# Splitting the second mixer's gated output once, with one token part kept on chip, and new instruction orders at part changes and at the kernel's end

## The chip, the cores and the metric

The kernel runs on one core of a Trainium2 chip. The core has five engines with an instruction stream each: TensorE (PE, the matmuls), VectorE (DVE), ScalarE (ACT), GpSimd (POOL) and SyncE (SP, which here only issues DMAs). They wait for one another through semaphores. POOL and ACT can issue DMAs too. The metric is the device time of one execution in microseconds; the time of a kernel is the median of its runs. Besides these, one execution was recorded by the hardware profiler.

## What is computed

One inference step of a two-layer streaming encoder over 1024 prompt and 32 sample frames (1056 tokens, model width 1024), all in fp32. The first layer mixes by retention, the second by gated linear attention (GLA); each is followed by a feed-forward stage with a causal convolution. Cut to what matters:

```python
for i in range(2):
    h = rmsnorm(x, norm_mix[i])
    if i == 0:
        y, S = retention_mixer(h, ...)   # (silu(g) * groupnorm(o)) @ w_out
    else:
        y, S = gla_mixer(h, ...)         # (silu(r) * rms(o) * norm_g) @ w_out
    x = x + y
    h = rmsnorm(x, norm_ffn[i])
    y, cs = conv_ffn(h, ...)             # (silu(gate) * val) @ w_down after w_up and the convolution
    x = x + y
return rmsnorm(x, norm_final), states
```

In GLA the decay of the keys is a logarithm of a sigmoid of a low-rank product (the "gate features" `a`, 16 wide, times `w_a2`), summed along the tokens.

## The kernel before

**Arithmetic.** An fp32 product is made of three matmuls: each operand is split into a high half, rounded to the engine's faster fp32r type, and a low half, the rest. A split is a copy on ACT (high) and a subtraction on DVE (low). `load_w` does it for weights: a DMA into a `raw` tile (512 KB, 128 x 1024), the copy `whi` and the subtraction `wlo`, both at L102. `Down` (L1187) does it for the other operand: a load into HR (L1221), a copy (L1223), a subtraction (L1224).

**Stages**, in order of time: the retention's input products, its four heads (until 712 us), its output product with w_ro (to about 882), the first feed-forward stage, GLA (1617 to 1947), GLA's output gate (w_gg, to 2039), its output product with w_go (to 2137), the second feed-forward stage and the last norm.

**Retention heads.** A head has eight pieces of prompt tokens and one of sample tokens. For each piece `output` computes the result `po` and its norm: statistics on DVE (L585, L586), a scale from them (L587, root on ACT at L589, L591 to L593), and the scaled result `on` on ACT (L599); `norm` transposes `on` on PE (L604, for the sample the tile is called `or`) and multiplies with the gate (L609). `update` computes the new state `Sn`: matmuls at L621, a DVE instruction at L629. In the last head `Down.early` (L1195) already loads and splits the first two k tiles of w_ro and of its other operand; L546 calls it for the second one.

**Down.** w_ro, w_go and the feed-forward's down product are run by `Down.run` in token parts: `CQ`, four parts of 264 tokens, for w_ro (16 k tiles) and w_go (8 k tiles); `CM`, parts of 384, 384 and 288, for the down product. In each part PE runs over the k tiles, and for each over eight output column tiles `nt`, with three matmuls each (L1248 to L1250). Three weight tiles (`keep`) stay on chip from part to part and are used first in the later parts; the others are loaded and split again in each part. At the last k tile each `nt` is evicted: DVE adds it to the residual (L1424 for w_ro and w_go, L1485 and L1516 for the down product), ACT squares it, and sums of squares are made on DVE and POOL (L148, L215). The norm of a part is computed while PE works on the next part (`hold`: how many k tiles the last column tile waits for its bank).

**Gate and w_go.** `second(1)` first computes, for eight tiles f, the gate product (L1404, `pg`), silu, and the product with GLA's output (L1407), and stores the result to DRAM (`scr_og`). w_go's `Down` reads it back, 32 loads of 132 KB, and splits it there.

**Up-projection.** `ffn_up` forms its products from seven instead of eight block products (numbered m). `weight_sums` and the operand sums (L288, L289, L293, L317 to L323, L312, L313) feed them; each unit's products go to PSUM banks named "a", "b", "c" (line 342), and `put` (L1311) adds them to the output rows. Products 2 and 4 share bank "b".

**Order.** A tile scheduler places the instructions by priority and by what is ready in its model; `order(a, b)` makes `a` stand behind `b`. `later` takes postponed work off a list. Around GLA's start the order follows the program: `qk_products`, `run_tails` (norm of the last part), `closers` (which release the feed-forward's rooms), `qk_out`, then `gates_in` (matmuls L1143 and L1144, feature tile `asb` at L1146 to L1149) and `gate` (L893, L897, L900, scan L902).

**Last norm.** `final_phase` squares the evicted tiles of the last part (L1524), adds them in pairs on POOL (L1528), reduces five tiles on PE (L219), computes the root on DVE and ACT (L225, L164 to L169), scales by `gcol` on ACT (L1511) and by the root on DVE and, for the last pair, POOL (L1537), and stores in four DMAs of 288 KB (L1538).

Of the kernel before, what the change touches and what calls it, by code (L numbers as in the profile page):

```python
# [9 lines left out]
F32 = mybir.dt.float32  # L10
# [40 lines left out]
def trunk_kernel(ctx: ExitStack, tc: tile.TileContext, io):  # L51
# [249 lines left out]
    def seven(X, wsrc, sm, snap_room, begin, put, first):  # L301
# [34 lines left out]
        def product(f, s, i, after):  # L336
            m = first.get((f, s), ORD)[i]
            if i == 0:
                unit[f, s] = {}
                begin(f, s)  # L340
            d = unit[f, s]
            bank = {1: "a", 6: "a", 7: "a", 2: "b", 4: "b", 5: "c", 3: "c"}[m]
            if bank not in d:
                d[bank] = sm("pu")
            ps = d[bank][:, :TH]
            wh, wl = W[f][m]
            x = X[s][m]
            for kt in range(4):
                k = slice(kt * P, kt * P + P)
                mm = PE.matmul(ps, wh[:, k], x[:, 0, kt], start=m in (1, 2, 4, 5) and kt == 0, stop=False,  # L350
                               skip_group_check=True)
# [61 lines left out]
    def retention():  # L413
# [50 lines left out]
        for h in range(RH):  # L464
# [5 lines left out]
            def before(m):  # L470
# [74 lines left out]
                if samp and h + 1 == RH:  # L545
                    d1s[0].early(1, split)  # L546
# [9 lines left out]
            def output(ctx):  # L556
# [20 lines left out]
                else:  # L577
# [9 lines left out]
                V.tensor_scalar(ab[:L, 0:1], mv[:L, 1:2], rcol[:L, h, 3:4], EPS,  # L587
                                op0=ALU.mult, op1=ALU.add)
# [23 lines left out]
                norms.append(norm)  # L612

            def update(ctx):
# [13 lines left out]
                if old is not None:  # L628
                    V.scalar_tensor_tensor(sn, old, float(GAMMA[h] ** L), pu, op0=ALU.mult, op1=ALU.add)  # L629
                else:  # L630
                    S.copy(sn, pu)
                st = sn
                if m >= 7:
                    dst = io["o_ret_p"] if m == 7 else io["o_ret_s"]
                    nc.sync.dma_start(dst[h].rearrange("(d p) e -> p d e", p=P), sn)

# [4 lines left out]
            for ctx in before(7), before(8):  # L641
                output(ctx)
                update(ctx)
# [212 lines left out]
    def gla(closers):  # L856
# [267 lines left out]
        asb = g1.tile([96, T], F32R, tag="asb", name="asb")  # L1124
        p00 = qk_products(0, 0)

# [3 lines left out]
        run_tails(lv)  # L1130
# [20 lines left out]

        units = [(h, c) for h in range(GH) for c in range(3)]
        gates_in(0)
        b00 = gate(*units[0])
# [35 lines left out]
    class Down:  # L1190
        def __init__(self, nk, wsrc, hsrc, chunks, res, sm, keep, hold):
            self.nk, self.wsrc, self.hsrc, self.chunks, self.res, self.sm = nk, wsrc, hsrc, chunks, res, sm
            self.hw = max(n for _, n in chunks)
            self.keep, self.hold, self.kept, self.ops = keep, hold, {}, {}
            self.banks = None  # L1195

        def early(self, kt, after=None):
# [10 lines left out]
            self.ops[0, kt] = load_w(self.wsrc(kt), None, after), (h, h[:, 512:])  # L1208

        def load(self, c, kt):  # L1210
# [16 lines left out]
        def run(self, room, evict, norm_a, norm_b, done, nxt=()):  # L1227
# [3 lines left out]
            for c, (c0, n) in enumerate(self.chunks):  # L1231
# [20 lines left out]
                for i, kt in enumerate(kts):  # L1252
# [118 lines left out]
    def second(l, scr, wg, wo, gncol, ntile, nxt):  # L1371
# [20 lines left out]
        AR = ear.enter_context(pool(f"ar{l}", side="right")).tile([P, 16 * TH + 4 * (T + 4)], F32, tag="AR", name=f"AR{l}")  # L1392
        if wg:
            gn = fp.tile([P, ntile], F32, tag="gn", name=f"gn{l}")
            nc.sync.dma_start(gn, gncol)
            gt = rooms(o=ring(0, T, 3, AR), sg=ring(3 * T, T, 3, AR))
            for f in range(ntile):
# [13 lines left out]
        with pool(f"xh{l}") as xhp, pool(f"xb{l}") as xbp:  # L1411
            XH = xhp.tile([P, 16 * TH], F32R, tag="XH", name=f"XH{l}")
            XB = xbp.tile([P, 32 * TH], F32R, tag="XB", name=f"XB{l}")
# [3 lines left out]
                         kw=ring(8 * TH, 2 * D, 3, XB), hh=ring(0, TH, 8, XH), hl=ring(8 * TH, TH, 8, XH))  # L1417
# [5 lines left out]
            def evict(c, nt, a, ps, ss):  # L1423
                V.tensor_tensor(a, a, ps, op=ALU.add)  # L1424
                sumsq(ss, nt, a, TH)
                c0, n = CQ[c]
                nc.sync.dma_start(scr_x[:, nt, c0:c0 + n], a)

# [80 lines left out]
    def final_phase(down, room, sm):  # L1509
        def scale_g(a, nt):  # L1510
            S.activation(a, a, AF.Copy, scale=gcol[:, 4, nt:nt + 1])  # L1511

        squares = []

        def evict(c, nt, a, ps, ss):
# [17 lines left out]
        def scale(c, xr, kt):  # L1533
            c0, n = CM[c]
            a = xr[:, kt:kt + 2]
            eng = G if c == 2 and kt == 6 else V
            eng.tensor_tensor(a, a, R[:, c0:c0 + n].unsqueeze(1).to_broadcast([P, 2, n]), op=ALU.mult)  # L1537
            (S if c == 2 and kt % 4 else nc.sync).dma_start(io["o_y"][:, kt:kt + 2, c0:c0 + n], a)  # L1538
# [117 lines left out]
_SCRATCH = {"scr_x5": (2, P, 2, 4, TH), "scr_q": (RH - 1, 4, P, 2, 2, TH), "scr_sg": (16, P, T),  # L1656
# [31 lines left out]
```

## Time and profile before

| quantity | value |
|---|---|
| median of 3 runs | 2870.28 us |
| lowest and highest run | 2870.03 and 2872.78 us |
| the profiled execution | 2871.84 us |
| its span, first to last instruction | 2870.1 us |
| mean granted PE clock | 0.996 |
| bytes moved by DMA | 361.40 MB |

A line of the profile names an engine, a source line (L1249), an operation and the tiles it writes and reads (`pd<-hh,whi`). Views used below: busy time of each engine; what an engine waited for; a timeline (start, duration, and in brackets the idle time before it and what released it); groups of instructions (count, busy time, mean in ns); and busy time in stretches of time that one chooses, with the PE clock that was granted.

### The profile page before, as it was taken

How to read it: one execution, taken by the hardware profiler on the slowest of the kernel's cores; microseconds unless marked ns; L12 is line 12 of the kernel's file. 1: busy time of each engine (PE TensorE's matmuls, PEld its weight loads, DVE VectorE, ACT ScalarE, POOL GpSimd, SP SyncE). 2: the span in 40 equal slices, each digit the busy share in tenths (PEclk: the TensorE clock that was granted, in tenths of full speed). 3: DMA queues.
4: the chain of work that ended last, by engine and by line, in shares of the span. 5: the costliest groups of instructions: out<-in, count | busy, mean ns of one | idle time of the engine just before them, and what ended most of it. 6: DMA issues, size and time to landing. Idle time of an engine off the chain costs nothing.

```text
span 2870.1 us, 51913 instructions
## 1 busy us (share of the span) xinstructions
PE 2815.3 (98%) x20648; PEld 2718.8 (95%) x20648; DVE 1975.2 (69%) x3329; ACT 1321.0 (46%) x2382; POOL 277.2 (10%) x521
## 2 busy tenths in 40 slices
PE   7999999999999999999999999999999999999998
PEld 7999988887999999999999999999999999999998
DVE  7676666666678877787555677774498777776544
ACT  5443444444554444444444555553354444444443
POOL 0000000000010111111000132220011111110000
PEclk9999999999999999999999999999999999999999
DMA  5333444433874222223755401115651222227544
GB/s 222 95 105 105 132 140 119 121 106 99 279 223 138 75 84 73 89 68 115 252 183 179 130 30 48 46 44 195 199 153 60 84 74 88 69 82 251 185 151 144
DMA packets 208227, 361.40 MB, mean 126 GB/s; under 512 B 35888, under 2 KB 146608, under 8 KB 207472
## 3 DMA queue, kind: packets, MB, share of 16 engines
q1 hardware_dynamic: 207152, 355.34, 38.8%
q8 instruction: 161, 2.64, 0.4%
q0 software_dynamic: 288, 2.16, 0.2%
q14 instruction: 82, 0.67, 0.1%
q10 hardware_dynamic: 544, 0.59, 0.1%
HBM read 276.91 MB, written 81.12 MB: 125 GB/s over the span
## 4 chain that ended last, share of the span: by engine, by line
PE 89%; DVE 7%; ACT 2%; issue 1%; DMA 1%; POOL 1%; DVEq 0%; SPq 0%; ACTq 0%; POOLq 0%
PE pu L355 13%; PE pu L350 13%; PE pu L354 13%; PE pd L1248 8%; PE pd L1249 8%; PE pd L1250 8%; PE psv L245 2%; PE psv L246 2%; PE psv L247 2%; PE pg L123 1%; PE pg L124 1%; PE pg L125 1%; PE pl L972 1%; PE pj L123 1%; PE pj L124 1%
## 5 line engine op out<-in xcount | busy, mean ns | idle before, releaser
L102 DVE TENSOR_TENSOR wlo<-raw,whi 128x1024 fp32r<-128x1024 f32 x226 | 282.1, 1251 | 229.2 <-ACT whi L102 218.5
L102 ACT CAST whi<-raw 128x1024 fp32r<-128x1024 f32 x226 | 235.8, 1048 | 284.4 <-PE pd L1249 212.8
L1248 PE MATMUL pd<-hh,whi 128*128 128x384 f32 (+1 forms) x880 | 284.9, 324 | 0.0
L1249 PE MATMUL pd<-hl,whi 128*128 128x384 f32 (+1 forms) x880 | 284.2, 323 | 0.1
L1250 PE MATMUL pd<-hh,wlo 128*128 128x384 f32 (+1 forms) x880 | 283.8, 323 | 0.0
L333 ACT COPY HR<-pu 128x264 f32<-128x264 f32 x264 | 98.9, 375 | 311.4 <-PE pu L355 308.9
L355 PE MATMUL pu<-XA,wgl 128*128 128x264 f32 x752 | 213.6, 284 | 0.0
L350 PE MATMUL pu<-XA,wgh 128*128 128x264 f32 x752 | 212.7, 283 | 0.0
L354 PE MATMUL pu<-XA,wgh 128*128 128x264 f32 x752 | 212.5, 283 | 0.0
L1331 DVE SCALAR_TENSOR_TENSOR AR<-AR,cw 128x1058 f32<-128x1058 f32 x88 | 116.0, 1318 | 72.8 <-ACT AR L1330 70.4
L1249 PEld LDWEIGHTS pd<-hl,whi 128*128 128x128 f32 x880 | 165.2, 188 | 0.9 <-DVE hl L1224 0.4
L1248 PEld LDWEIGHTS pd<-hh,whi 128*128 128x128 f32 x880 | 165.2, 188 | 0.4
L1250 PEld LDWEIGHTS pd<-hh,wlo 128*128 128x128 f32 x880 | 165.2, 188 | 0.1
L1249 PE MATMUL pd<-XH,whi 128*128 128x264 f32 x560 | 158.9, 284 | 1.7 <-DVE XH L1224 1.6
L1250 PE MATMUL pd<-XH,wlo 128*128 128x264 f32 x560 | 158.9, 284 | 0.0
L1248 PE MATMUL pd<-XH,whi 128*128 128x264 f32 x560 | 158.8, 286 | 0.0
L313 DVE TENSOR_TENSOR wtl<-rv,wth 128x1024 fp32r<-128x1024 f32 x58 | 71.0, 1225 | 117.0 <-ACT wth L312 112.8
L1311 DVE TENSOR_TENSOR AR<-HR,pu 128x264 f32<-128x264 f32 (+2 forms) x440 | 144.8, 368 | 4.6 <-PE pu L355 4.6
L350 PEld LDWEIGHTS pu<-XA,wgh 128*128 128x128 f32 x752 | 141.2, 188 | 0.0
L354 PEld LDWEIGHTS pu<-XA,wgh 128*128 128x128 f32 x752 | 141.2, 188 | 0.0
L355 PEld LDWEIGHTS pu<-XA,wgl 128*128 128x128 f32 x752 | 141.1, 188 | 0.0
L350 PE MATMUL pu<-XA,wsh 128*128 128x264 f32 x464 | 132.3, 285 | 2.3 <-DVE ARi L773 1.0
(465 smaller groups left out, 9592.4 us busy)
## 6 DMA issues: line engine op xcount, KB each, us to landing
raw<-w_down SPq DMA_DIRECT2D x120, 512.0 KB, 3.7
raw<-w_ro SPq DMA_DIRECT2D x55, 512.0 KB, 4.8
rg<-w_up SPq DMA_DIRECT2D x44, 512.0 KB, 3.5
rv<-w_up SPq DMA_DIRECT2D x44, 512.0 KB, 3.6
scr_h<-AR SPq DMA_DIRECT2D x44, 512.0 KB, 2.6
HR<-scr_h SPq DMA_DIRECT2D x84, 192.0 KB, 3.7
raw<-w_go SPq DMA_DIRECT2D x23, 512.0 KB, 3.8
scr_x<-AR SPq DMA_DIRECT2D x64, 132.0 KB, 4.4
```

Source lines behind the costliest of these rows:

```text
L102: ins = S.copy(hi, raw), V.tensor_tensor(lo, raw, hi.bitcast(F32), op=ALU.subtract)
L123: PE.matmul(ps, hi[:, k], rh, start=kt == 0, stop=False)
L313: V.tensor_tensor(l_, src, h.bitcast(F32), op=ALU.subtract)
L333: S.copy(t, b)
L350: mm = PE.matmul(ps, wh[:, k], x[:, 0, kt], start=m in (1, 2, 4, 5) and kt == 0, stop=False, skip_group_check=True)
L354: PE.matmul(ps, wh[:, k], x[:, 1, kt], start=False, stop=False, skip_group_check=True)
L355: mm = PE.matmul(ps, wl[:, k], x[:, 0, kt], start=False, stop=kt == 3, skip_group_check=True)
L1248: PE.matmul(o, w[0][:, k], h[0][:, :n], start=i == 0, stop=False)
L1249: PE.matmul(o, w[0][:, k], h[1][:, :n], start=False, stop=False)
L1250: self.last_mm = PE.matmul(o, w[1][:, k], h[0][:, :n], start=False, stop=i == nk - 1)
L1311: V.tensor_tensor(u[:, d:d + n], t[:, o:o + n], b[:, o:o + n], op=op)
L1331: V.scalar_tensor_tensor(cj, uj[:, 1:T + 3], cw[:, nt, 1:2], cj, op0=ALU.mult, op1=ALU.add)
```

## The change

Six edits:

1. Each retention head's end is written out: the prompt's last state update is placed behind the first step of its norm (`ts`). In the last head the second early k tile of w_ro is moved behind the last piece's output and update: the operand split behind the root and `ts`, the weight split behind the root and `Sn`, and the next weight split behind `on` and `Sn`.
2. In w_ro and w_go the DVE part of the first weight split after a part's evictions is placed behind the last eviction (`self.after`).
3. In the first unit of each up-projection product 4 gets a bank of its own, "d".
4. GLA's gated output is split in the gate stage. The first token part goes into XH on chip; the other three are stored split in a new DRAM tensor `scr_hg` and loaded by w_go's `Down` in groups of four k tiles, 1056 KB each, from POOL's queue. The kept weights of w_go are k tiles 0 to 2 instead of 2 to 4.
5. At GLA's start the first gate features are computed ahead of the query and key product and of the tail of the norm.
6. `final_phase` adds the squares of tiles 4 to 7 on DVE, reduces four tiles instead of five, places the scaling by `gcol` behind the last square or the exponential of the root, and scales and stores the last two tiles singly, all on DVE.

```diff
@@ ffn_up's products
             bank = {1: "a", 6: "a", 7: "a", 2: "b", 4: "b", 5: "c", 3: "c"}[m]
+            if m == 4 and first and f == s == 0:
+                bank = "d"
...
-                    put(f, 1, s, 0, ALU.subtract, d[3], d["b"])
+                    put(f, 1, s, 0, ALU.subtract, d[3], d[4])
             elif m == 4:
-                d[4] = True
+                d[4] = ps
@@ retention head
-                if samp and h + 1 == RH:
-                    d1s[0].early(1, split)
...
-            def update(ctx):
+            def update(ctx, after=None):
...
-                    V.scalar_tensor_tensor(sn, old, float(GAMMA[h] ** L), pu, op0=ALU.mult, op1=ALU.add)
+                    ins = V.scalar_tensor_tensor(sn, old, float(GAMMA[h] ** L), pu, op0=ALU.mult, op1=ALU.add)
+                    if after is not None:
+                        order(ins, after)
...
-            for ctx in before(7), before(8):
-                output(ctx)
-                update(ctx)
+            c7, c8 = before(7), before(8)
+            root7, ts7, on7 = output(c7)
+            sn7 = update(c7, ts7)
+            if h + 1 == RH:
+                d1s[0].early(1, (root7, ts7), (root7, sn7))
+                d1s[0].after = on7, sn7
+            output(c8)
+            update(c8)
@@ GLA's start
-        asb = g1.tile([96, T], F32R, tag="asb", name="asb")
-        p00 = qk_products(0, 0)
...
-        run_tails(lv)
...
-        for f in closers:
-            f()
-        g2 = es.enter_context(pool("g2", side="right"))
-        q00 = qk_out(0, p00)
+        asb = g1.tile([96, T], F32R, tag="asb", name="asb")
...
+        gates_in(0)
+        p00 = qk_products(0, 0)
+        q00 = qk_out(0, p00)
+        b00 = gate(0, 0)
+        run_tails(lv)
+        for f in closers:
+            f()
+        g2 = es.enter_context(pool("g2", side="right"))
         units = [(h, c) for h in range(GH) for c in range(3)]
-        gates_in(0)
-        b00 = gate(*units[0])
         gates_in(1)
         gates_in(2)
@@ Down
             if kt not in self.keep:
-                w = load_w(self.wsrc(kt))
+                w = load_w(self.wsrc(kt), None, self.after)
+                self.after = None
...
+            if self.groups:
+                q, k = divmod(kt, 4)
+                if (c, q) not in self.groups:
+                    h = self.room("hq").rearrange("p (k j t) -> p k j t", k=4, j=2)
+                    G.dma_start(h, io["scr_hg"][c - 1, q])
+                    self.groups[c, q] = h
+                h = self.groups[c, q]
+                self.ops[c, kt] = w, (h[:, k, 0], h[:, k, 1])
+                return
...
                             if i == nk - 1:
-                                evict(c, nt, xr[:, nt], ps[nt][:, :n], ss)
+                                put = evict(c, nt, xr[:, nt], ps[nt][:, :n], ss)
+                                self.after = put and (None, put)
@@ second: gate stage
+            gt = rooms(o=ring(0, T, 3, AR), sg=ring(3 * T, T, 3, AR), t=(XB, [8 * TH + 4 * D, 0], 6 * TH))
+            hg = [XH[:, q * 8 * TH:(q + 1) * 8 * TH].rearrange("p (k j t) -> p k j t", k=4, j=2) for q in range(2)]
+            d1s[l].groups = {(0, q): h for q, h in enumerate(hg)}
...
                 V.scalar_tensor_tensor(sg, o, gn[:, f:f + 1], sg, op0=ALU.mult, op1=ALU.mult)
-                nc.sync.dma_start(scr[f], sg)
+                t = gt("t").rearrange("p (c j t) -> p c j t", c=3, j=2)
+                sv = sg.rearrange("p (c t) -> p c t", c=4)
+                for h, l_, v in ((hg[f // 4][:, f % 4, 0], hg[f // 4][:, f % 4, 1], sv[:, 0]),
+                                 (t[:, :, 0], t[:, :, 1], sv[:, 1:])):
+                    S.copy(h, v)
+                    V.tensor_tensor(l_, v, h.bitcast(F32), op=ALU.subtract)
+                nc.sync.dma_start(io["scr_hg"][:, f // 4, :, f % 4].rearrange("c p j t -> p c j t"), t.bitcast(F32))
@@ final_phase
-            S.activation(sq, a, AF.Square)
-            if nt % 2 == 0 or nt == 7:
-                squares.append(sq)
-            else:
-                G.tensor_tensor(squares[-1], squares[-1], sq, op=ALU.add)
+            squares.append(sq)
+            last_sq[0] = S.activation(sq, a, AF.Square)
+            if nt in (1, 3):
+                G.tensor_tensor(squares[nt - 1], squares[nt - 1], sq, op=ALU.add)
+            if nt == 7:
+                for k in (4, 6):
+                    V.tensor_tensor(squares[k], squares[k], squares[k + 1], op=ALU.add)
...
-        norm(2, squares)
-        for nt in (6, 7, 0, 1, 2, 3, 4, 5):
-            scale_g(xr[:, nt], nt)
-        for kt in (6, 0, 2, 4):
-            scale(2, xr, kt)
+        norm(2, squares[0::2])
+        for nt in range(KT):
+            order(scale_g(xr[:, nt], nt), last_sq[0] if nt < 4 else last_r[0])
+        for kt, m in ((0, 2), (2, 2), (4, 2), (6, 1), (7, 1)):
+            scale(2, xr, kt, m)
...
-           Down(8, lambda k: io["w_go"][k], lambda k: scr_o[1][k], CQ, scr_x, None, range(2, 5), 4)]
+           Down(8, lambda k: io["w_go"][k], lambda k: scr_o[1][k], CQ, scr_x, None, range(0, 3), 4)]
```

More of the change, by code (lines that the diff above doesn't have):

```diff
@@ L612, in output @@
                 norms.append(norm)
-            def update(ctx):
+                return last_root, ts, last_on
+            def update(ctx, after=None):
                 nonlocal st
@@ L635, in update @@
                     nc.sync.dma_start(dst[h].rearrange("(d p) e -> p d e", p=P), sn)
+                return ins
             for m in range(7):
@@ L1194, in __init__, with early @@
             self.keep, self.hold, self.kept, self.ops = keep, hold, {}, {}
-            self.banks = None
-        def early(self, kt, after=None):
+            self.banks = self.after = self.groups = None
+        def early(self, kt, after=None, wafter=None):
             c0, n = self.chunks[0]
@@ L1207, in early @@
                     order(a, b)
-            self.ops[0, kt] = load_w(self.wsrc(kt), None, after), (h, h[:, 512:])
+            self.ops[0, kt] = load_w(self.wsrc(kt), None, wafter or after), (h, h[:, 512:])
         def load(self, c, kt):
@@ L1392, in second @@
         AR = ear.enter_context(pool(f"ar{l}", side="right")).tile([P, 16 * TH + 4 * (T + 4)], F32, tag="AR", name=f"AR{l}")
+        ex = ExitStack()
+        XH = ex.enter_context(pool(f"xh{l}")).tile([P, 16 * TH], F32R, tag="XH", name=f"XH{l}")
+        XB = ex.enter_context(pool(f"xb{l}")).tile([P, 32 * TH], F32R, tag="XB", name=f"XB{l}")
         if wg:
@@ L1407, in second @@
                 V.scalar_tensor_tensor(sg, o, gn[:, f:f + 1], sg, op0=ALU.mult, op1=ALU.mult)
-                nc.sync.dma_start(scr[f], sg)
+                t = gt("t").rearrange("p (c j t) -> p c j t", c=3, j=2)
[5 more added lines that the diff above has]
+                nc.sync.dma_start(io["scr_hg"][:, f // 4, :, f % 4].rearrange("c p j t -> p c j t"), t.bitcast(F32))
             ln_exp_table(last_silu[0])
         down = Down(NF, lambda k: io["w_down"][l, k], lambda k: scr_h[k], CM, scr_x, sm, range(6, 9), 3)
-        with pool(f"xh{l}") as xhp, pool(f"xb{l}") as xbp:
-            XH = xhp.tile([P, 16 * TH], F32R, tag="XH", name=f"XH{l}")
-            XB = xbp.tile([P, 32 * TH], F32R, tag="XB", name=f"XB{l}")
+        with ex:
             X = x_room([(XB, 0), (XB, 1), (XB, 2), (XB, 3), (XH, 0), (XH, 1)])
             rest = rooms(xr=(AR, [16 * TH, 24 * TH, 8 * TH, 0], 8 * TH), hr=ring(0, TH, 4, HR),
-                         kw=ring(8 * TH, 2 * D, 3, XB), hh=ring(0, TH, 8, XH), hl=ring(8 * TH, TH, 8, XH))
+                         kw=ring(8 * TH, 2 * D, 3, XB), hh=ring(0, TH, 8, XH),
+                         hl=ring(8 * TH, TH, 8, XH), hq=ring(0, 8 * TH, 2, XH))
             def droom(name):
@@ L1423, in evict @@
             def evict(c, nt, a, ps, ss):
-                V.tensor_tensor(a, a, ps, op=ALU.add)
+                ins = V.tensor_tensor(a, a, ps, op=ALU.add)
                 sumsq(ss, nt, a, TH)
@@ L1427, in evict @@
                 nc.sync.dma_start(scr_x[:, nt, c0:c0 + n], a)
+                return ins
             def norm(c, ss, after=None):
@@ L1510, in scale_g @@
         def scale_g(a, nt):
-            S.activation(a, a, AF.Copy, scale=gcol[:, 4, nt:nt + 1])
-        squares = []
+            return S.activation(a, a, AF.Copy, scale=gcol[:, 4, nt:nt + 1])
+        squares, last_sq = [], [None]
         def evict(c, nt, a, ps, ss):
@@ L1523, in evict, with scale @@
             sq = (ss[nt] if nt < 2 else room("sq"))[:, :n]
-            S.activation(sq, a, AF.Square)
-            if nt % 2 == 0 or nt == 7:
-                squares.append(sq)
-            else:
-                G.tensor_tensor(squares[-1], squares[-1], sq, op=ALU.add)
+            squares.append(sq)
[5 more added lines that the diff above has]
+                    V.tensor_tensor(squares[k], squares[k], squares[k + 1], op=ALU.add)
         def norm(c, ss):
             rms_row(ss, *CM[c], sm("pn"), None, c < 2)
-        def scale(c, xr, kt):
+        def scale(c, xr, kt, m=2):
             c0, n = CM[c]
[L1535 to L1538, printed above, removed]
+            a = xr[:, kt:kt + m]
+            V.tensor_tensor(a, a, R[:, c0:c0 + n].unsqueeze(1).to_broadcast([P, m, n]), op=ALU.mult)
+            (S if c == 2 and kt % 4 else nc.sync).dma_start(io["o_y"][:, kt:kt + m, c0:c0 + n], a)
         def done(c, xr):
```

9 lines of the change are left out of this document (4 added, 5 removed).

## The prediction

> **What bounds the kernel now.** I read the page's busy times first, then its chain that ended last.
>
> ```profile
> PE 2815.3 (98%) x20648; PEld 2718.8 (95%) x20648; DVE 1975.2 (69%) x3329; ACT 1321.0 (46%) x2382; POOL 277.2 (10%) x521
> PE 89%; DVE 7%; ACT 2%; issue 1%; DMA 1%; POOL 1%; DVEq 0%; SPq 0%; ACTq 0%; POOLq 0%
> ```
>
> TensorE (PE) is busy 2815.3 of 2870.1 us. The change keeps its matmuls (20,119 instead of 20,120 in the kernels' instruction orders), so it can win only part of the 55 us in which PE stands still, and of the stretches in which PE is busy at half clock. The third view, what PE waited for, splits the first (columns: us in all, times, longest):
>
> ```profile
> PE pn L717 <- DVE rr L169: 13.1, 2, 10.5
> PE pu L350 <- DVE AR L1311: 6.2, 4, 4.1
> PE pt L604 <- ACT on L599: 3.4, 1, 3.4
> PE pd L1248 <- DVE AR L1424: 2.0, 2, 1.2
> PE pd L1249 <- DVE XH L1224: 1.6, 1, 1.6
> PE pj L893 <- DVE asb L1149: 1.6, 1, 1.6
> PE pj L123 <- DVE t L897: 0.6, 1, 0.6
> ```
>
> The first row is the kernel's start, which the change leaves alone. The other six are each met by one part of it. Not in that list are the tail after the last matmul and the half-clock stretches behind the larger stops. The fourth view, busy time by stretch (us; busy us and instructions of PE, PEld, DVE, ACT, POOL; granted PE clock, DMA share, GB/s), shows those:
>
> ```profile
> 712.50:716.00 3.50, 3.46 (x16) 3.46 (x17) 1.14 (x4) 2.13 (x3) 0.33 (x2) 0.51 0.93 313
> 1640.90:1644.40 3.50, 3.50 (x13) 3.50 (x12) 3.35 (x6) 2.02 (x8) 2.87 (x3) 0.51 0.00 0
> 2144.00:2149.50 5.50, 5.17 (x23) 5.20 (x24) 4.88 (x6) 2.94 (x3) 0.00 (x0) 0.50 0.23 58
> 2149.50:2155.00 5.50, 5.50 (x44) 5.37 (x43) 3.47 (x7) 2.23 (x5) 0.00 (x0) 1.00 0.38 136
> 2858.50:2870.10 11.60, 1.09 (x5) 0.53 (x3) 5.13 (x7) 2.77 (x7) 1.91 (x1) 0.69 0.30 102
> ```
>
> At clock 0.50 a 264-column matmul takes 5.17/23 = 0.22 us, at 1.00 it takes 5.50/44 = 0.125. So 3.5 us at half clock cost at most 1.7 us, and less where PE would have waited anyway.
>
> **The change part by part.**
>
> *Last retention head.* Rows of the end of the retention (start, duration):
>
> ```profile
> 705.23 1.22 DVE L102 TENSOR_TENSOR wlo<-raw,whi 128x1024 fp32r<-128x1024 f32 x1
> 707.10 1.20 DVE L629 SCALAR_TENSOR_TENSOR Sn<-Sn,pu 128x1024 f32<-128x1024 f32 x1
> 708.32 1.19 DVE L102 TENSOR_TENSOR wlo<-raw,whi 128x1024 fp32r<-128x1024 f32 x1
> 711.71 0.78 ACT L599 ACTIVATE on<-po,ab 128x512 f32<-128x512 f32 x1 [1.61 <-DVE ab L593]
> 712.54 1.11 PE L604 MATMUL pt<-ident,on 128*128 128x128 f32 x4 [3.45 <-ACT on L599]
> 716.85 0.43 PE L604 MATMUL pt<-ident,or 32*128 32x32 f32 x4
> ```
>
> DVE does two weight splits and the state update Sn between the pieces of the norm that `on` waits for. After the change the norm's first steps go first and the splits behind them: some 3 us leave the chain, and the transposes of `on` come at about 709.5 (estimate: 712.54 less 2.4 for the two splits and part of Sn). But the sample's transposes of `or` come 18 matmuls (2.2 us) later, and their norm now stands behind Sn and the moved split; the raw tile of that split is also loaded later on SP, behind the state's store. I place `or` at about 715.2 instead of 716.85, so 1.7 us are won at that point. The new wait there, 2.5 to 3 us, can bring back a half-clock stretch. Bounds: 0 (half clock costs all) to 3.4 (no new wait). I take 1.0, nearer the low end, because the next wait is seen in the instruction order. The same swap in the three other heads touches waits of 0.35 us each, and I set it at 0 within 1 us either way.
>
> *Evictions before the next part's weight splits.* The two stops in the row for L1424 (2.0 us) lie between the third and fourth part of w_ro, where DVE and ACT split the next part's weights between evictions. Those splits now follow the last eviction. They are covered: three kept weight tiles feed the next part first, three times some 2.9 us (24 matmuls of 0.12). The later splits of 1.2 us each must then fit one per 2.9 us. Gain 1.9; bounds -1 (one split late) to 2.0.
>
> *Second mixer's gated output split once.* These groups of the w_go stage (us 2040 to 2137; count, busy, mean ns), and the mixer's gate stage ahead of it:
>
> ```profile
> L1224 DVE TENSOR_TENSOR XH<-HR,XH 128x264 fp32r<-128x264 f32 x25 | 11.5, 462 | 8.9 <-ACT XH L1223 8.9
> L1223 ACT CAST XH<-HR 128x264 fp32r<-128x264 f32 x25 | 10.0, 411 | 17.2 <-DMA HR<-scr_og 15.4 <-PE pd L1250 1.6
> ```
>
> ```profile
> 1947.00:2039.00 92.00, 92.00 (x580) 91.55 (x579) 40.47 (x61) 26.49 (x36) 0.00 (x0) 1.00 0.58 197
> 2110.00:2137.00 27.00, 25.34 (x204) 24.71 (x203) 26.57 (x45) 14.71 (x25) 6.29 (x12) 1.00 0.47 144
> ```
>
> 32 casts and 32 subtractions of 264 columns, and 32 loads, leave the w_go stage. Its last part is where DVE is full (26.57 of 27.00 us), and the 1.6 us stop (XH L1224) lies there; without these subtractions it goes. Gain 1.6, bounds 0 to 1.6. In their place the gate stage gets, for each of 8 tiles, a cast and a subtraction of 264 columns and of 792. By the 462 and 411 ns above and three times that for the wide ones, this is at most 8 x 1.85 = 15 us on DVE and 8 x 1.65 = 13 us on ACT, beside 92 us of unbroken PE with 51 us of DVE and 65 us of ACT free. It costs nothing there; without that cover it would be 15 us.
>
> What is new is that parts 1 to 3 are loaded by six transfers of 1056 KB from POOL's queue, which stood idle here. Each waits until PE has finished the half (four k tiles) whose room it takes, and is needed about 10.4 us later: four k tiles are 4 x 24 x 0.12 = 11.5 us, less the matmuls of the eighth column tile that come late. In POOL's order the additions of squares stand behind these waits, and the row norm waits for them, but they are due a whole part later. The nearest row is POOL's only other load, of the same size:
>
> ```profile
> XA<-scr_x POOLq DMA_DIRECT2D x2, 1056.0 KB, 6.9
> 347.00:354.00 7.00, 7.00 (x60) 7.00 (x59) 5.86 (x8) 1.82 (x3) 0.70 (x1) 1.00 0.96 307
> ```
>
> The first of the two landed while the DMA engines were 96% busy and DVE 84%, so 3 us are left and I cost the loads at 0. Bounds: 0 to a stall of 3.4 us each if landing doubles to 13.8. The Trainium skill (SBUF — State Buffer, SBUF: two separate sides) warns that a DMA issued from GpSimd starves while DVE holds the shared port in a two-port mode, since its descriptors cannot be written. In the row above DVE was busy and the load still landed, so the trace does not bear out a long delay for DVE's work there; by that rule the stall of the rival below would come first in the last part.
>
> *A bank of its own for the first unit's fourth product.* At the start of the second up-projection:
>
> ```profile
> 2139.54 1.60 DVE L289 TENSOR_TENSOR XB<-AR,XB 128x1056 fp32r<-128x1056 f32 x1
> 2143.76 0.42 DVE L1311 TENSOR_TENSOR AR<-HR,pu 128x264 f32<-128x264 f32 x1
> 2145.89 1.22 DVE L313 TENSOR_TENSOR wsl<-rg,wsh 128x1024 fp32r<-128x1024 f32 x1 [0.51 <-ACT wsh L312]
> ```
>
> PE waits 4.1 us for the eviction at 2143.76, which stands behind L289 and three half sums. Now product 4 needs not wait for it and PE's order there changes. The next thing needed is the weight sum behind the row at 2145.89, and DVE reaches it some 3 us sooner with no splits left in w_go. I count about 3.7 us of idle time in place of 4.06 and 2.5 smaller stops, all starting earlier: gain 2.9, bounds 0 (PE is fed by DVE for the next 30 us, so it may lose it again) to 4.1. In the first up-projection PE's order stays: 0.
>
> *Gate features first in the second mixer.*
>
> ```profile
> 1635.39 0.96 DVE L902 TENSOR_TENSOR_SCAN b<-smask,t 128x384 f32<-128x384 f32 x1
> 1638.69 0.64 DVE L1149 TENSOR_TENSOR asb<-asr,asb 32x384 fp32r<-32x384 f32 x1
> 1647.41 0.60 DVE L897 TENSOR_SCALAR t<-pj,ba 128x384 f32<-128x384 f32 x1
> ```
>
> The scan can end some 3.9 us earlier, at about 1632.4 instead of 1636.35. PE's first stop (L1149, 1.6) stays about as long, because `asb` of the second part is now queued behind three products that wait for POOL and ACT. What PE reaches next waits for L897, which now stands behind two products and a q more (0.35 + 0.35 + 0.54): 1646.3 instead of 1648.0. Gain 1.7, of which a half-clock stretch may take some: 1.5, bounds -1 to 3.9.
>
> *Last head and end.* The end, after the last matmul:
>
> ```profile
> 2859.63 0.46 DVE L225 TENSOR_SCALAR rm<-pn 128x288 f32<-128x288 f32 x1 [2.62 <-PE pn L219]
> 2860.12 0.44 ACT L164 ACTIVATE rt<-rm 128x288 f32<-128x288 f32 x1 [0.48 <-DVE rm L225]
> 2860.47 0.52 ACT L1511 ACTIVATE AR<-AR,gcol 128x288 f32<-128x288 f32 x1
> 2862.90 3.30 DVE L1537 TENSOR_TENSOR AR<-AR,R 128x576 f32<-128x576 f32 x3
> 2863.00 1.91 POOL L1537 TENSOR_TENSOR AR<-AR,R 128x576 f32<-128x576 f32 x1 [5.18 <-issue]
> ```
>
> Squares go back to back, one reduction (two passes) leaves PE, and the last pair is added on DVE: L225 comes about 1.0 us sooner. The scaling at 2860.47 no longer stands inside the root (0.3). DVE takes all scaling, without POOL beside it: 3 x 0.7 + 2 x 0.45 = 3.0 against 3.3. The last store is half as long. Together 1.7; bounds 0.7 (the norm's part alone is won) to 2.2 (1.2 MB at some 350 GB/s need 3.4 us).
>
> Sum: 1.0 + 1.9 + 1.6 + 2.9 + 1.5 + 1.7 = 10.6 us. The profiled execution took 2871.84 us (span 2870.1 and 1.7 around it), which is 1.56 above the median 2870.28. So 2861.2 in a profile, and 2860 for the median.
>
> **The rivals.**
>
> *The waits come back.* The sample's norm, the weight sum and the chain behind the scan take what the three starts win. Then 1.9 + 1.6 + 1.7 = 5.2 are left: 2865. For it: all three have a next wait close behind, on the same DVE. Against it: these chains start earlier as well.
>
> *POOL's loads late (slower).* Place: w_go, from the first moment that landing takes over 10.4 us. At 13.8 six stalls of 3.4 make 20 us, and up to 1.7 each at half clock 10 more: 2880 to 2890. Against it stand 6.9 us and a DMA share of 0.47 in the last part; for it, that POOL's queue never carried such loads beside 512 KB weight loads in w_go.
>
> *Clock never halves.* If the stops at 712, 1640 and 2140 become too short or too split, the rows at 0.51 and 0.50 vanish: 1.7 + 1.7 + 2.6 = 6.0 instead of the 1.4 or so that my terms hold: 2855. The Trainium skill (TensorE: Matmul & The Clock Gate, Part 1) says that about 3.4 us without work halve the clock, and 3.4 us of work release it. The stop of 1.6 us at 1638 was followed by half clock, so the trace shows it for shorter stops, and I give this little.
>
> **How the numbers follow.** Forecast 0.56, waits come back 0.20, late loads 0.13, clock never halves 0.11. A change of under 0.2% (5.7 us, so 2864.6 to 2876.0) counts as none. Faster: 0.54 of the forecast, 0.11, and 0.07 of the first rival: 0.72. Same: 0.02 and 0.12: 0.14. Slower: the late loads and 0.01 of the forecast: 0.14. The terms' bounds taken halfway give 2854 to 2867; the range reaches to 2870 to hold the first rival. The forecast's own range is 2856 to 2864.
>
> **What would show it.** Right: no row for L1424, for XH L1224 or for `on` L599 among PE's waits; a short new one for the sample's `or`, one for wsh L312 instead of L1311; six POOL loads landing in 6 to 9 us; a tail of under 10 us. Wrong: PE waiting in w_go for a load or for a weight split, or a stop of over 3 us at 714, 1636 or 2140 with the clock at 0.5 behind it.

## The result, and the profile after

| | before | changed |
|---|---|---|
| median | 2871.66 us (20 runs, 2870.03 to 2876.15) | 2879.07 us (20 runs, 2875.53 to 2883.05) |
| ratio | 1 | 1.0024, 95% interval 1.0017 to 1.0031 |
| profiled execution, span | 2871.84, 2870.1 | 2883.05, 2881.3 |

The change made the kernel some 7 us slower, where 10 us faster were forecast. The profiled execution of the changed kernel is one of its longest, so its trace shows more loss (11.2 us) than the medians (7.4). Cut at the first or last matmul of each stage, the two spans differ in these places (the first row runs from the second head's first product to w_ro's last, at 905 us in the kernel before, not at about 882 as the section on the stages has it):

| stage, us | before | changed | difference |
|---|---|---|---|
| second to fourth retention head and w_ro | 474.0 | 482.3 | +8.3 |
| GLA | 329.7 | 328.2 | -1.5 |
| w_go | 97.2 | 104.5 | +7.3 |
| second up-projection | 460.4 | 459.7 | -0.8 |
| from the last product's end to the end | 13.6 | 12.2 | -1.4 |

All others agree within 0.1 us, but for 0.7 us less ahead of the first row. So two stages lose 15.6 us, and they are the two in which edit 2 acts. What PE waited for in the changed kernel between 700 and 880 us (the heads' end and w_ro up to its last part), and then between 2040 and 2150 us (w_go); columns: us in all, times, longest:

```profile
PE pd L1269 <- DVE rm L225: 6.8, 2, 4.8
PE pt L604 <- ACT or L599: 1.4, 1, 1.4
PE pd L1269 <- DVE Sn L630: 1.0, 1, 1.0
PE pd L1269 <- DVE AR L1457: 1.0, 1, 1.0
PE pt L604 <- ACT on L599: 0.6, 1, 0.6
```

```profile
PE pd L1269 <- DVE rm L225: 5.0, 3, 2.8
PE pd L1271 <- DVE wlo L102: 0.4, 2, 0.2
```

The rows for `on` (3.4 before) and for XH in w_go (1.6) have shrunk or gone as forecast; of the row for the evictions (2.0) half is left. A row that the kernel before did not have stands in their place: PE waits 11.8 us in all for `rm` at L225, the first step of a part's norm. `rm` frees the PSUM bank into which the sums of squares were reduced, and the eighth column tile of the new part is waiting for that bank.

Why `rm` is late is seen on DVE and SP at w_ro's first part change. DVE's timeline, first before, then changed (start, duration, count at the end; in brackets idle time and releaser):

```profile
758.13 1.22 DVE L102 TENSOR_TENSOR wlo<-raw,whi 128x1024 fp32r<-128x1024 f32 x1 [0.78 <-ACT whi L102]
...
759.62 1.78 DVE L1424 TENSOR_TENSOR AR<-AR,pd 128x264 f32<-128x264 f32 x5
...
766.66 1.23 DVE L102 TENSOR_TENSOR wlo<-raw,whi 128x1024 fp32r<-128x1024 f32 x1 [1.02 <-ACT whi L102]
...
772.53 0.43 DVE L225 TENSOR_SCALAR rm<-pn 128x264 f32<-128x264 f32 x1 [3.40 <-PE pn L219]
```

```profile
760.35 0.42 DVE L1457 TENSOR_TENSOR AR<-AR,pd 128x264 f32<-128x264 f32 x1
760.69 4.64 DVE L102 TENSOR_TENSOR wlo<-raw,whi 128x1024 fp32r<-128x1024 f32 x3
...
772.39 1.23 DVE L102 TENSOR_TENSOR wlo<-raw,whi 128x1024 fp32r<-128x1024 f32 x1 [6.03 <-ACT whi L102]
774.27 1.23 DVE L102 TENSOR_TENSOR wlo<-raw,whi 128x1024 fp32r<-128x1024 f32 x1 [0.66 <-ACT whi L102]
775.41 0.43 DVE L225 TENSOR_SCALAR rm<-pn 128x264 f32<-128x264 f32 x1
```

Before, three splits are done ahead of the evictions (the last of them is shown) and two more by 767.9, so that L225 starts as soon as PE has reduced the squares (pn L219). In the changed kernel the three splits follow the last eviction (760.69, three of them in 4.64 us), and the next two stand in DVE's order ahead of L225. DVE sits 6 us idle in front of the first of them, because its weight has not landed. L225 could have run in that time, since PE had reduced the squares by 769.6:

```profile
769.03 0.61 PE L219 MATMUL pn<-ss,ones 128*128 128x264 f32 x2
```

SP's queue shows why the weight is late, before and then changed:

```profile
757.15 0.61 SPq L100 DMA_DIRECT2D raw<-w_ro  x1
760.07 5.87 SPq L1427 DMA_DIRECT2D scr_x<-AR  x8
766.07 0.35 SPq L100 DMA_DIRECT2D raw<-w_ro  x1
```

```profile
759.12 8.14 SPq L1460 DMA_DIRECT2D scr_x<-AR  x8
767.38 1.33 SPq L100 DMA_DIRECT2D raw<-w_ro  x3
...
773.64 2.21 SPq L100 DMA_DIRECT2D raw<-w_ro  x2
```

There are three raw tiles. Before, weight loads go out up to 757 us, ahead of the eight stores of the part's result. With all three raw tiles held until the evictions are over, none can go out before those stores, and the next three wait until 767.38. ACT gets the first at 771.3. PE's clock is halved in the second half of this stop and after it, and again after three other stops (busy time by stretch, columns as in the prediction):

```profile
771.10:773.50 2.40, 0.00 (x0) 0.00 (x0) 1.11 (x1) 1.35 (x2) 0.00 (x0) 1.00 0.96 382
773.60:775.90 2.30, 0.01 (x1) 0.01 (x1) 1.58 (x3) 0.64 (x1) 0.00 (x0) 0.50 0.70 178
775.90:780.40 4.50, 4.50 (x20) 4.50 (x21) 3.43 (x10) 3.44 (x7) 0.00 (x0) 0.50 0.69 221
876.00:879.40 3.40, 3.40 (x18) 3.40 (x17) 2.66 (x8) 2.84 (x7) 0.00 (x0) 0.50 0.73 214
2084.30:2087.70 3.40, 3.40 (x18) 3.40 (x17) 3.29 (x9) 1.49 (x2) 0.79 (x2) 0.50 0.73 200
2111.60:2115.00 3.40, 3.40 (x16) 3.40 (x17) 2.39 (x6) 1.57 (x3) 0.31 (x1) 0.50 0.79 281
```

A row whose stretch is partly at half clock shows an average, so the stretches here are cut where the clock changes. PE works at 0.50 for 4.5 us after the first stop and for 3.4 us after each of the others: 2.0 us for L225 at w_ro's third part change, 1.9 and 2.8 in w_go. With busy x (1 - clock) that is 2.3 + 3 x 1.7 = 7.4 us lost to the clock, on top of the 11.8 us of waiting. The two account for the 15.6 us of the two stages: 19.2, less 7.1 that the stages won (2.8 at `on`, 1.0 at the evictions, 1.6 at XH, and 1.7 by the half-clock stretch at 712 us, which is gone), and 2.8 for the new small waits (`or` 1.4, Sn 1.0, wlo 0.4), make 14.9.

The loads from POOL's queue, which the prediction gave as the way to lose time, are not part of it. Their row in the changed kernel's DMA issues from 2046 to 2150 us (count, KB each, median us to landing):

```profile
XH<-scr_hg POOLq DMA_DIRECT2D x6, 1056.0 KB, 7.0
```

What the other five edits are worth cannot be read off here, since the loss in two stages lies over their gains.

### The profile page after: what moved, and what is told of

Read it like the earlier page. It is cut to its first block, busy times and chain, and to the rows that moved or that the text cites. A ratio compares the mean times of both kernels' runs of the same rounds, so it can differ in the third digit from the quotient of the medians.

```text
span 2881.3 us, 51803 instructions
## 1 busy us (share of the span) xinstructions
PE 2820.0 (98%) x20646; PEld 2722.1 (94%) x20646; DVE 1972.9 (68%) x3317; ACT 1321.9 (46%) x2366; POOL 286.9 (10%) x525
## 4 chain that ended last, share of the span: by engine, by line
PE 60%; DVE 5%; issue 3%; ACT 1%; DMA 1%; POOL 0%; DVEq 0%; POOLq 0%; ACTq 0%; SPq 0%
PE pu L357 10%; PE pu L352 10%; PE pu L356 10%; PE pd L1269 6%; PE pd L1270 6%; PE pd L1271 6%; PE pl L982 1%; PE pj L123 1%; PE pv L245 1%; PE pv L246 1%; PE pj L124 1%; PE pj L125 1%; PE pv L247 1%; DMA raw<-w_go 1%; PE pg L123 1%
```

## The experiments

Two theories at first. A: edit 2 is the loss, by way of the held raw tiles and L225 behind the late splits. B: the loads that edits 1 and 4 moved crowd the DMA engines, so that weights land late.

**e1: without edit 2.**

```diff
-                                put = evict(c, nt, xr[:, nt], ps[nt][:, :n], ss)
-                                self.after = put and (None, put)
+                                evict(c, nt, xr[:, nt], ps[nt][:, :n], ss)
```

> The changed kernel without edit 2: the first weight split after a part's evictions is no longer placed behind the last eviction; all other edits stay. Theory A (edit 2 holds the three raw weight tiles until the evictions are over, so the next weight loads are issued late, and the norm's row L225 stands on DVE behind the splits of these late weights): the stops of 4.8, 1.0 and 2.0 us in w_ro and of 1.9 and 2.8 us in w_go go, w_ro takes 192 to 195 us instead of 204.1 and w_go 95 to 97 instead of 104.5, and the median is 2859 to 2863 us. Theory B (the loads that edits 1 and 4 moved crowd the DMA engines, and weights land late because of them): the stops in w_go stay, w_go takes over 102 us and the median is over 2872 us.

Measured: median 2868.35 us (11 runs) beside 2871.97 of before, ratio 0.999 (0.9981 to 0.9999); w_go 98.1 us instead of 104.5, heads and w_ro together 472.9 instead of 482.3. Theory B falls. The other five edits together are worth 3.6 us here. The median is some 5 us above what was expected of theory A (and w_go 1 us), since the old waits return and some are longer. Rows of this run, w_ro first (700 to 870 us), then w_go and what follows (2036 to 2175 us):

```profile
PE pd L1269 <- DVE AR L1456: 2.3, 2, 1.5
```

```profile
PE pd L1269 <- DVE rm L225: 1.4, 1, 1.4
...
PE pd L1269 <- DVE AR L1456: 1.2, 1, 1.2
```

The evictions wait again (2.3 us in w_ro, 1.2 in w_go). In this run's timelines the wait ends behind a square that stood on ACT behind a weight cast (at w_ro's first part change also behind an operand cast that waited 0.7 us for its load), as it did in the kernel before at w_ro's third part change.

**e2: edit 2 alone on the kernel before.** The diff is that of `Down.load`'s `self.after`, of the line above, and of the returned instruction in `evict`.

> The kernel before with edit 2 alone. Theory A: w_ro gets a stop of 4 to 5 us at its first part change and is 8 to 12 us longer than 192.1; w_go also gets stops of 2 to 3 us, and the median is 2882 to 2892 us. Theory B: without the moved loads edit 2 does what it is written for, the 2.0 us of stops at the third part change of w_ro go, and the median is 2868 to 2870 us.

Measured: 2880.04 us (8 runs), ratio 1.0027 (1.0017 to 1.0037). Heads and w_ro 477.0 us, w_go 102.1. So edit 2 alone costs as much as the whole change, some 2 us less than the least that was expected of theory A; theory B, which expected a gain, falls again. By stages the loss is seen in w_go (4.9 us, with stops of 2.5 us for a weight split and 1.8 for L225); 477.0 us for heads and w_ro is no more than another kernel took there without edit 2 (e7, below). At the first part change of w_ro the stop is only 1.4 us instead of 4 to 5 (w_ro is 2 us longer instead of 8 to 12), though SP issues the loads at the same time:

```profile
767.47 1.32 SPq L100 DMA_DIRECT2D raw<-w_ro  x3
```

and L225 starts at 774.9 (775.4 in the changed kernel). What differs is PE: it comes to the part change at 773.95 us in this kernel and at 771.1 in the changed one, because edit 1 lets w_ro start 5.1 us earlier there (708.8 instead of 713.9), of which 2.9 us are left at the part change. They were waited for again.

**e4: the changed kernel with the norm row ahead of the late splits.** Edit 2 stays, and so do the held tiles.

```diff
+                    self.row = dg[0] if not norm_b and J + 2 <= i < J + 4 else None
                     self.load(c, kt)
...
-                w = load_w(self.wsrc(kt), None, self.after)
+                w = load_w(self.wsrc(kt), None, self.after or (self.row and (None, self.row)))
```

Here `dg[0]` is the instruction of L225, which `rms_row` and `norm` now return.

> The changed kernel with one order more: in w_ro and w_go the DVE part of the seventh and eighth weight split of a part is placed behind the norm's row L225 of the part before. The raw tiles are still held and the loads still late. Theory A in its full form (PE waits because L225 stands behind the late splits, not because it needs these weights yet): the five stops go or fall under 0.5 us and the median is 2859 to 2864 us. Theory A in a weaker form (the late weights themselves are what PE needs): the stops only move to waits for whi or wlo and the median stays over 2872 us. Theory B: no change against 2879 us, within 3.

Measured: 2867.89 us (11 runs), ratio 0.9988 (0.9979 to 0.9997). DVE at the same part change in this run:

```profile
768.20 0.43 DVE L225 TENSOR_SCALAR rm<-pn 128x264 f32<-128x264 f32 x1 [2.60 <-PE pn L219]
771.01 1.23 DVE L102 TENSOR_TENSOR wlo<-raw,whi 128x1024 fp32r<-128x1024 f32 x1 [2.38 <-ACT whi L102]
772.66 1.23 DVE L102 TENSOR_TENSOR wlo<-raw,whi 128x1024 fp32r<-128x1024 f32 x1 [0.42 <-ACT whi L102]
```

The weights come as late as before, but L225 no longer waits for them, and PE has no stop at that part change. The 11.2 us between the changed kernel and this one are thus a matter of one instruction's place in a queue. Two stops are left besides those at the last head, 1.9 us for the evictions at the third part change of w_ro and 2.7 us for a weight split in w_go: in w_go the late weight itself is what PE needs, so the weaker form of theory A holds in that one place. The median is 4 us above the full form's range. It is level with that of e1, which has no edit 2 at all (2868.35): with the order mended, edit 2 does no harm, and no gain of it shows in the medians.

**The other edits.** The next runs price them. Stages that a kernel does not touch vary between profiles: heads and w_ro took 474.0, 475.3 and 477.0 us in three kernels with the same code there, GLA 329.6 to 331.3 in six, w_go 97.1 to 97.5 in five, the second up-projection 459.4 to 460.8 in four, the tail 13.6 to 14.1 in six. A difference counts only beyond that.

**e5: run e4 without edit 4, and e6: edit 4 alone on the kernel before.**

> The kernel of run e4_norm_row_first without edit 4 (w_go reads and splits the gated output as before). Theory C (splitting once removes the stop of 1.6 us in w_go's last part but brings others of the same size, since the freed engines' work only moves: SP's and POOL's big loads come between the weight loads): w_go takes 97 to 100 us as with it, and the median stays within 2 us of 2867.9. Rival D (splitting once is worth the predicted 1.6 us or more): w_go takes over 101 us and the median is over 2870 us.

> The kernel before with edit 4 alone. Theory C: w_go takes 97 to 99 us (97.2 before), the stop for XH in the last part is replaced by one for the norm row or a weight split, and the median is 2870 to 2873 us. Rival D: w_go takes 95.0 to 96.0 us, no new stop, median 2868.5 to 2870. Rival of the prediction (POOL's loads late): stops for a POOL load, over 100 us.

Measured: e5 2869.42 us (ratio 0.999, 0.9981 to 0.9999), w_go 98.8 us, second up-projection 461.3. e6 2869.49 us (0.9996, 0.9987 to 1.0006), w_go 98.3, second up-projection 457.8. The two theories are not told apart: in e5 w_go and the median are where C has them, but the 1.5 us between its median and e4's are also the size of the forecast gain; in e6 w_go is where C has it and the median where D has it, and its interval reaches over 1. By stages edit 4 alone costs 1.1 us in w_go and wins 2.6 just behind it (1.6 against the shortest of the untouched kernels). The two stages together took 556.1 us, against 556.8 to 557.9 in the kernel before, e8, e10 and e11, which leave both as they were: 0.6 to 1.8 us. The waits of e6 from 2036 to 2180 us:

```profile
PE pu L350 <- DVE AR L1322: 4.1, 2, 2.7
PE pd L1259 <- DVE AR L1446: 1.4, 1, 1.4
PE pd L1259 <- DVE rm L225: 1.4, 1, 1.4
```

The stop for XH is gone and two of 1.4 us have come, for an eviction and for L225, so DVE stays the limit there (busy for 26.89 of the 27.00 us from 2110). The stop at the start of the up-projection falls from 4.1 to 2.7 us. Neither in e6, which has these loads alone, nor in e1, which lacks edit 2, did anything wait for POOL's loads.

**e7: edit 3 alone (bank "d").**

> The kernel before with edit 3 alone. If the weight sum wsh is what PE needs next (as the changed kernel's stop of 4.4 us for it says), the stop of 4.1 us is only renamed: the second up-projection takes 459.5 to 460.5 us (460.45 before) and the median is 2870 to 2873. If the bank was the limit, as predicted: 457 to 458 us, and 2867 to 2870.

Measured: 2874.00 us (ratio 1.0008, 0.9999 to 1.0017); second up-projection 461.2 us. Its waits from 2120 to 2190 us:

```profile
PE pu L352 <- ACT wsh L312: 5.7, 1, 5.7
```

The stop of 4.1 us for the bank is now one of 5.7 us for the weight sum. PE leaves product 4 earlier and comes to the next operand, which is no earlier. Renamed, not removed; the stage and the median are even a little above the ranges that were expected of this.

**e8: edits 1, 5 and 6; e10: edit 1 alone; e11: edit 1 without its last line** (`d1s[0].after = on7, sn7`).

> The kernel before with edits 1, 5 and 6 (last retention head, gate features first, end). By the stages of the changed kernel these are the parts that gain: some 2 to 3 us at the last head, 1.5 in GLA, 1.35 in the tail, so 2865.5 to 2868 us. If the gain at the last head is given back within w_ro (a stop of 1.5 us at its first part change was seen in run e1_no_evict_order), 2868 to 2869.5 us.

> The kernel before with edit 1 alone. Theory: the 3.7 us won at the heads' end are given back in w_ro, where the part changes get stops of 1.5 us: heads and w_ro together 473.5 to 475 us (474.0 before), median 2870.5 to 2872.5 us. As predicted (1.0 us won): 472.5 to 473.5.

> Edit 1 alone without its last line, which places the next weight split behind `on` and `Sn`. If that order gives back the gain (it delays the raw tile and the loads behind it), heads and w_ro together take 471 to 472.5 us and the stop at w_ro's first part change is under 0.5 us. If the give-back comes from PE reaching the part change earlier, the stop stays at 1.5 us and the sum at 473.5 to 475.

Measured: e8 2869.78 us (0.9994, 0.9985 to 1.0003), e10 2874.45 (1.0007, 0.9998 to 1.0016), e11 2872.28 (1.0000, 0.9991 to 1.0009). The span up to w_ro's first product is 3.5 to 3.7 us shorter in each, but heads and w_ro together take 474.5, 473.5 and 474.8 us, against 474.0 to 477.0 without edit 1. Their waits for evictions in w_ro grow, as e11's row from 700 to 880 us shows (2.0 us, two times, before):

```profile
PE pd L1256 <- DVE AR L1432: 4.1, 4, 1.3
```

The new ones lie at w_ro's first part change: 1.5 to 2.2 us in e1, e8, e10 and e11, which have edit 1 without edit 2, and none in the kernels without edit 1 (before, e6, e7) or in those that have edit 1 and edit 2 with the norm row first (e4, e5, e9). So edit 1 gives back much of what it wins, and its last line is not the reason, as e11 has the same. At the third part change, for which edit 2 was made, the waits vary from 0.8 to 2.7 us without it (2.0 in the kernel before) and from 0.4 to 1.9 with it, so no gain of it is shown there. The medians of e8 and e10 came out above the ranges expected of them. GLA with edit 5 took 328.1 to 328.2 us in five of six kernels (331.3 in e5), the tail with edit 6 12.2 to 12.6 in six.

**e9: a combination.** Edits 1, 4, 5 and 6; edit 2 in w_ro only, with the norm row first as in e4; no edit 3.

```diff
-                                self.after = put and (None, put)
+                                self.after = put and (None, put) if nk > 8 else None
...
+                    self.row = dg[0] if nk > 8 and not norm_b and J + 2 <= i < J + 4 else None
```

> Edits 1, 4, 5 and 6, with edit 2 in w_ro only and there with the norm row ahead of the seventh and eighth weight split (as in run e4_norm_row_first); w_go without edit 2; no edit 3. By the stages of the runs so far: heads and w_ro 471 to 472 us (474.0 before), GLA 328.2 (329.7), w_go and the second up-projection 556 together (557.7), tail 12.2 (13.6): a profile of 2863 us and a median of 2863 to 2866.5 us, below both kernels. If the gains at w_go and w_ro do not add up, 2867 to 2869.

Measured: 2866.50 us (11 runs, 2862.69 to 2870.78) beside 2871.65 of before, ratio 0.998 (0.9971 to 0.9989). It is faster than both kernels, at the upper end of what was expected, and not told apart from e4 (2867.89) and e1 (2868.35). Heads and w_ro took 473.2 us, more than expected, GLA 328.1, w_go and the second up-projection 556.4, the tail 12.2. The first up-projection, which nothing in this kernel changes, took 2.1 us more than in the kernel before, with a half-clock stretch at 931 us.

## Why the prediction was wrong, point by point

**The step that failed** is "Evictions before the next part's weight splits", with its gain of 1.9 us and a worst case of 1 us lost. It looked at the third part change of w_ro, where the two stops were, and asked only whether the splits themselves would be done before PE needs them. It did not follow what the splits hold. Three raw tiles stay occupied through all evictions, so the next loads move behind eight stores on SP, and the two splits that wait for these loads stand ahead of L225 on DVE. Measured: 11.8 us of stops for L225 and 7.4 us of half clock in the changed kernel; 8.1 us between the medians for edit 2 alone (e2), 10.7 between those of the changed kernel and e1. Beside the 1.9 forecast, that step makes 12.6 of the 18 us between forecast and result; the other five terms, 8.7 together in the forecast, came to 3.6 (e1). The order on DVE was there to be read: in the kernel before, too, two splits stand ahead of L225. It was harmless as long as the weights were early.

**The rivals.** The slower side was given to POOL's loads, at 2880 to 2890 us. The time came near, the mechanism was not there: landing took 5.1 to 8.2 us and nobody waited. "The waits come back" was right in part: `on` gave way to `or` (1.4) and Sn (1.0), and the bank to wsh.

**Last retention head** (1.0 forecast): w_ro starts 3.7 us sooner, but without edit 2 (e8, e10, e11) heads and w_ro together stand between 0.8 us over and 3.5 us under the kernels without the edit. A gain of 1.0 is not contradicted and not shown. The new wait was placed only half: besides `or`, a wait for Sn (1.0) and the first part change took it. The half-clock stretch that was feared there did not come back in the changed kernel.

**Gated output split once** (1.6): the stop for XH went as forecast, the gate stage hid the new splits (92.71 us in both), and the loads cost nothing. But the stage is bound by DVE at its end, so 1.1 us was lost there and the gain showed in the next stage. Net 0.6 to 1.8 us by stages, not resolved by the medians.

**Bank "d"** (2.9): nothing. The term was wrong in kind: what freed the time in the sum was DVE's lighter load, which belongs to edit 4 (e6 has it without edit 3), and the wait only changed its name (e7).

**Gate features first** (1.5): 1.5 us between the two profiles, about 2 against the middle of the unchanged kernels, and 1.4 to 1.6 between kernels that have no half-clock stretch in GLA (329.6 and 329.8 in e11 and e6 without the edit, 328.2 in the changed kernel, e1 and e4 with it). The scan ends 3.1 us sooner after the end of the down product (15.7 instead of 18.8 us after it), 3.9 were forecast. The waits came out otherwise: the one for `asb`, forecast to stay at 1.6, fell to 0.2, that for L897 went, and 1.6 us of others came (`asr` 1.3, q 0.3). So the size is right and the sum behind it only in part; that it fits to 0.1 us is luck.

**End** (1.7): 1.4 to 1.5. DVE's rows of the changed kernel answer to those of before:

```profile
2871.37 0.46 DVE L225 TENSOR_SCALAR rm<-pn 128x288 f32<-128x288 f32 x1 [0.84 <-PE pn L219]
...
2874.36 2.83 DVE L1572 TENSOR_TENSOR AR<-AR,R 128x576 f32<-128x576 f32 x5
```

L225 starts 2.3 us after the end of the main products (2869.06); before it was 3.1 (2856.51 to 2859.63). The scaling takes 2.83 us instead of 3.30 (3.0 forecast). This mechanism held.

**The clock.** The forecast let PE's half-clock stretches shrink with the stops. Two of the three did go, at the last head and at GLA's start; the one at the second up-projection stayed, and four new ones came with the new stops. The Trainium skill (TensorE: Matmul & The Clock Gate, Part 1) speaks of an idle window of about 3.4 us; the stops of 1.9 and 2.8 us in w_go were followed by 3.4 us at 0.50, so here shorter stops were enough.

**The range.** Halfway to the terms' bounds it is some 1.5 to 2.5 us wider at each end than its own working: the terms sum to 10.6 us and their bounds to -1.3 and 17.2 (the loads' stall and the three other heads left out), so halfway lie 4.7 and 13.9 us, that is 2856 to 2866 us and not 2854 to 2867.

What stays open: why w_ro's first part change waits for evictions when PE arrives earlier (e8, e10, e11) was read from the waits and not tried by itself, and neither was a fourth raw tile.

## What to carry to other kernels

An order that makes a producer wait also holds its input buffer: before placing a split or cast later, follow the buffer back to the load that needs it next, and see which stores that load then queues behind. Then look at what stands behind the late consumer in each engine's order; a short instruction that frees a bank belongs ahead of work that waits for a transfer. An order inside a loop acts at every turn of it: this one was written for one part change of one stage and cost most at others. A gain at the end of one stage should be booked only where the next stage's bound lets it through.

## What was not expected of the hardware

GLA's wait for L897, 0.6 us in the kernel before, was 2.1 us in e2, e6, e10 and e11, whose instructions there are the same. The waits of e2 from 1600 to 1700 us:

```profile
PE pj L123 <- DVE t L897: 2.1, 1, 2.1
PE pj L893 <- DVE asb L1149: 1.6, 1, 1.6
```

The wait ahead of it is 1.6 us in both. The clock decides between 0.6 and 2.1. In the kernel before PE runs at half clock between the two waits (1640.9 to 1644.4, in the prediction's rows); in e6, where GLA starts at the same 1617.4 us, the same stretch has the full clock, and L897 starts at the same time as before (1647.41 there):

```profile
1640.90:1644.40 3.50, 3.50 (x22) 3.50 (x21) 3.35 (x6) 2.05 (x8) 2.87 (x3) 1.00 0.00 0
```

```profile
1647.42 0.60 DVE L897 TENSOR_SCALAR t<-pj,ba 128x384 f32<-128x384 f32 x1
```

The faster PE only waits 1.5 us longer for the same DVE instruction. So this half-clock stretch cost nothing: GLA took 329.7 us before and 329.8 in e6. Where the stretch fell later it did cost: GLA took 330.8 and 330.9 us in e10 and e2 (half clock from 1648.8 and 1651.2) and 331.3 in e5 (6.8 us of it from 1649.8). The 1.7 us that the rival of a clock that never halves counts for the stretch at 1640.9 were therefore not there to be won. What places a half-clock stretch in one execution and not in another was not tried. It makes equal code differ by 1 to 3 us in a stage, which is why edits of 1 us are read here by several profiles together.
